# Input tiles normed in pairs, modulation steps of four narrow products, and separate gate and branch entries in a two-layer mixer trunk

## The chip, the cores and the metric

The kernel runs on one core of one Trainium2 chip. A core has five engines with an instruction stream each: TensorE (PE in the profile; PEld is its weight load), VectorE (DVE), ScalarE (ACT), GpSimd (POOL) and SyncE (SP, which issues the transfers). The metric is the device time of one execution in microseconds (us).

## The reference, cut to what matters

Two layers work on 512 latent tokens and 256 context tokens, 1024 channels wide. Each layer modulates a normed input, sends it through one wide projection to three branches (a gated delta rule, RG-LRU, neighbourhood attention), gates and merges the branches, and adds the projected sum back.

```python
for l in range(DEPTH):
    shift_l, scale_l, gate_l = jnp.split(silu_c @ w_mod[l] + b_mod[l], 3, axis=-1)
    shift_c, scale_c, gate_c = jnp.split(silu_cc @ w_mod[l] + b_mod[l], 3, axis=-1)
    h_lat = rms_norm(x, g_pre[l]) * (1.0 + scale_l[:, None]) + shift_l[:, None]
    h_ctx = rms_norm(ctx, g_pre[l]) * (1.0 + scale_c) + shift_c
    y_lat, y_ctx = hybrid_mixer(h_lat, h_ctx, ...)
    x = x + gate_l[:, None] * rms_norm(y_lat, g_post[l])
    if not last:
        ctx = ctx + gate_c * rms_norm(y_ctx, g_post[l])
# in hybrid_mixer:
p_lat, p_ctx = h_lat @ w_in, h_ctx @ w_in      # 3 branches' inputs, gates z, merge gates
merged = (gates[..., 0, :] * (ya @ w_branch[0])
          + gates[..., 1, :] * (yb @ w_branch[1])
          + gates[..., 2, :] * (yc @ w_branch[2]))
return merged @ w_out
```

## The kernel before, in words

**Tiling.** The 768 tokens are six tiles of 128: tiles 0 to 3 are latent, 4 and 5 context. The normed and modulated input `h` is kept transposed (channels on partitions) as a pair of fp16 halves, high and low. A weight chunk of 128 output columns arrives in fp32 in a ring of three raw buffers (`raw_t`), ACT casts its high half (`whi_...`), DVE subtracts to get the low half (`wlo_...`), and each chunk is then 24 matmuls of 512 latent columns (high by high, high by low, low by high over eight blocks of channels) and, where the context needs it, 24 of 256. A branch chunk (`b`) has half as many.

**Order.** Generators write the program. A planner, `Flow`, resumes whichever generator it holds ready by its own estimates of times, and so fixes a written order for each engine; on the chip every engine follows that order strictly. The main generator of a layer walks through the tokens of `schedule(l)` (L208): the inputs of the delta rule (`a`) and of attention (`k`, `q`, `v`), the branch gates (`z`, `za`, `zb`), the RG-LRU inputs (`xb`), the merge gates (`g`, each followed at once by its branch chunk `b`), and `("out",)`, at which the output weights are requested. Background generators (the delta rule, RG-LRU, attention, merging) fill in between. In the traces the projection of token `g` in layer 1 is called `1_g`, and the first three chunks of a layer, whose tokens are taken early, are called `f`, `f1`, `f2` (with `c` for context).

**Modulation.** `silu(c)` and `silu(c_ctx)` are the two real columns of the 32-column stationary operand `sc`. One part of a layer's `w_mod` is 8 steps: a 512 KB transfer `wm`, then two fp32 products of 512 columns into `pm` (L483), each in one group of 32 PSUM partitions. The steps run one at a time between projections. Parts 0 and 1 (shift and scale) of layer 1 are computed in layer 0's `g` 2 phase, part 2 (the output gate) of each layer in its `g` 0 phase by `gate_rows` (L534). All take their `wm` buffers from the same ring of three as the weight chunks. For layer 0 the startup computes shift and scale in four quarters of 256 columns (`pmq`, L667), each a 2 MB piece of `w_mod`.

**Startup.** `startup` (L587) fetches constants, the six input tiles `xt`, one weight chunk, quarter 0 of `w_mod`, two more chunks and quarters 1 to 3. Tiles are squared on ACT and scaled on DVE in a group of two and a group of four (`tiles_`, L632), transposed in fp32 (`xTp`, L266), and when all are transposed, `quarter` 0 starts, then 1 to 3 after one another; each gives shift and scale (`sa`, `sb`) for a quarter of the channels, `h` for them, and a quarter of the products `f`.

**RG-LRU and out stage.** `rg_core` (L861) runs one chain for each of four `j` (conv, two block-diagonal products `lru`, gates, scans on DVE), and yields `yb`, on which the branch products `b` 1 wait. After the merge, `out_tiles` (L1540) multiplies the merged pair `mg` by the output weights (`py`, 48 products of 512 columns for a tile), and `out_tail` (L1493) norms each tile, adds the residual and, in layer 0, squares and norms again (`normed`, L568), transposes (`xTp` from `sq`) and writes `h` for layer 1. A tail does its additions only when the tails before the previous one have ended, and its transposes only when the previous one has.

Of the kernel before, what the change touches and what calls it, by code (L numbers as in the profile page):

```python
# [17 lines left out]
P = 128  # L18
D = 1024
# [188 lines left out]
def schedule(l):  # L208
# [25 lines left out]
def build(tc, A, out):  # L234
# [133 lines left out]
    class Weights:  # L368


        def __init__(self):
            self.seq, self.raw, self.pair, self.more, self.n = [], [], [], None, 0
            for l in range(DEPTH):
                for t in schedule(l):
                    if len(t) > 1:
                        self.seq.append((A["w_in"][l, chunk_of(t)], KD, (l,) + t))
                    if t[0] == "g":
                        self.seq.append((A["w_branch"][l, t[1], t[2]], 4, (l, "b") + t[1:]))
# [94 lines left out]
    def mod_rows(l, part, fin, load):  # L473


        nxt_ = load(l, part, 0)
        yield nxt_
        pm = pst(f"pm{l}_{part}", [P, 512], keep=True)
        for k in range(KD):
            raw = nxt_  # L480
            for n in range(2):
                g = 32 * (2 * n + k % 2)
                nc.tensor.matmul(pm[g:g + 32, :], sc[:, k, :], raw[:, n, :], start=k < 2, stop=k >= KD - 2,  # L483
                                 tile_position=(0, g))
            fl.product(pm, 1.02)
            fl.drop(raw)
            fl.used[raw.name] = fl.now
            if k < KD - 1:
                nxt_ = load(l, part, k + 1)
                yield nxt_  # L490
# [37 lines left out]
    def wload(l, part, k):  # L528
        raw = raw_t([P, 2, 512], "wm")
# [4 lines left out]
    def gate_rows(l, pp, out_, rowt):  # L534
# [26 lines left out]
        yield from mod_rows(l, 2, fin, wload)  # L561
# [6 lines left out]
    def normed(pp, xt, dst=None):  # L568

        jk = pp.tile([P, D], F16, tag="jk", name="jk")  # L570
        ss = small.tile([P, 2], F32, tag="nss", name="nss")
        for i, hf in enumerate((slice(0, 512), slice(512, D))):
            S.activation(jk[:, hf], xt[:, hf], AF.Square, accum_out=ss[:, i:i + 1])
# [4 lines left out]
        sq = dst if dst is not None else pp.tile([P, D], F32, tag="xo", name="sq", bufs=4)  # L578
# [8 lines left out]
    def startup(mod, firsts):  # L587


        with tc.tile_pool(name="n0", bufs=1) as pp:  # L590
# [32 lines left out]
            fl.spawn(lru_rates(), 0)  # L623
# [8 lines left out]
            def tiles_(ts):  # L632

                n_ = len(ts)
                ss = pp.tile([P, 4, 2], F32, tag="xss", name="xss", bufs=6)[:, :n_]
                r = pp.tile([P, 4], F32, tag="xr", name="xr", bufs=6)[:, :n_]
                for i, t in enumerate(ts):
                    yield fl.until(xts[t])
                    for n in range(2):
                        jk = pp.tile([P, 512], F16, tag="jk", name="jk")  # L640
                        S.activation(jk, xts[t][:, n * 512:(n + 1) * 512], AF.Square, accum_out=ss[:, i, n:n + 1])
# [3 lines left out]
                rsqrt(r, ss[:, :, 0], n_, "l4")  # L645
                for i, t in enumerate(ts):
                    V.tensor_scalar(xts[t], xts[t], r[:, i:i + 1], None, op0=OP.mult)
                for t in ts:
                    yield fl.until(xts[t])
                    for q in range(2):  # L650
# [4 lines left out]
                        copy(xT[:, 4 * q:4 * q + 4, t * P:(t + 1) * P], pt)  # L655

            def quarter(q, before):
                yield before
                yield from fl.room()
                pm = pst("pmq", [P, 256], keep=True)  # L660
                for k in range(KD):
                    raw = raws[q, k - k % 2]
                    if k % 2 == 0:
                        yield fl.until(raw)
# [4 lines left out]
                    fl.product(pm, 0.5)  # L669
                row = pp.tile([P, 256], F32, tag="row", name="row")  # L670
                S.activation(row, pm, AF.Copy)
                fl.drop(pm)
                yield fl.until(row)
# [3 lines left out]
                for s, sl in enumerate((slice(0, SEQ), slice(SEQ, NT))):  # L677
                    if s == 1:
                        pass
                    for k in (2 * q, 2 * q + 1):  # L680
                        (V, G)[s].tensor_scalar(xT[:, k, sl], xT[:, k, sl], mod["sa"][:, k, s:s + 1],
                                        mod["sb"][:, k, s:s + 1], op0=OP.mult, op1=OP.add)
# [4 lines left out]
            xt_ = [fl.spawn(tiles_(ts), 1) for ts in ((0,1),(2,3,4,5))]  # L687
            ready, begun = {}, set()
# [11 lines left out]
            ws = []  # L700
            for wn in firsts:
                ws.append((yield from W.take(wn)))
            os_ = [pair_t("f0"), (lat_t("f1"), pst("f1c", [P, CTX], keep=True)),
                   (pst("f2", [P, SEQ], keep=True), pst("f2c", [P, CTX], keep=True))]
            for q in range(4):
                ks = (2 * q, 2 * q + 1)
                for s in range(2):
                    yield lambda: (q, s) in ready
                    yield ready[q, s] - fl.now
                    for w, o in zip(ws, os_):  # L710
# [27 lines left out]
    def layer(l, mod, first):  # L738
# [309 lines left out]
        def merge_in(mp, mg, br, m, o, t, first_, final, before):  # L1048
# [8 lines left out]
            if final:  # L1057
# [5 lines left out]
                                       op0=OP.mult, op1=OP.subtract)  # L1063

# [428 lines left out]
        def out_tail(pp, t, py, xt, gg, h, nmod, before):  # L1493

            jk = pp.tile([P, D], F16, tag="jk", name="jk")
            ss = small.tile([P, 2], F32, tag="nss", name="nss")
            for hf in range(2):
                S.activation(jk[:, hf * 512:(hf + 1) * 512], py[hf], AF.Square, scale=1.0 / SW,
# [5 lines left out]
            yield ended(*before[:-1])  # L1504
            xo = pp.tile([P, D], F32, tag="xo", name="xo", bufs=4)
            for hf in range(2):
# [3 lines left out]
                V.tensor_tensor(xo[:, cols], xo[:, cols], xt[:, cols], OP.add)  # L1510
# [313 lines left out]
```

## Time and profile before

| | |
|---|---|
| median of 3 runs | 1702.24 us (1702.2 to 1704.13) |
| the profiled execution | 1702.02 us, of which its span 1700.3 us |
| mean granted TensorE clock | 0.992 |
| PE busy | 1628.7 us, 96% of the span |
| PEld, DVE | 1026.5 us (60%), 1203.6 us (71%) |
| ACT, POOL | 886.9 us (52%), 270.1 us (16%) |
| moved | 139.80 MB, mean 82 GB/s |

The span is that of the engines' first to last instruction; what lies around it is 1.72 us. Busy times are shares of one execution; they overlap between engines. PE is busy nearly throughout, so the sums in the text count the time that it waits and the work that it does.

### The profile page before, as it was taken

The page shows a single profiled execution, that of the slowest core. Times are in us where ns is not written, and L with a number is a line of the kernel's source. Part 1 is how long each engine was busy: PE and PEld are TensorE (multiplying, and loading weights), DVE is VectorE, ACT ScalarE, POOL GpSimd, SP SyncE. Part 2 cuts the span into 40 slices and gives each one's busy share as a digit, 9 for nine tenths or more (in the row PEclk, how much of TensorE's full clock was granted, in tenths as well). Part 3 has the DMA queues.
Part 4 walks back from the last instruction along what each step waited for, and adds up shares of the span by engine and source line. Part 5 has one row for each costly group of instructions (what it writes and reads, how often), then busy time and mean ns, then how long its engine had stood idle before and what let it go on. Part 6 is the DMA issues. An engine that isn't in the chain of part 4 may idle for free. (4 is left out here: it accounts for less than half of the span.)

```text
span 1700.3 us, 30340 instructions
## 1 busy us (share of the span) xinstructions
PE 1628.7 (96%) x11452; PEld 1026.5 (60%) x11452; DVE 1203.6 (71%) x2866; ACT 886.9 (52%) x2130; POOL 270.1 (16%) x420
## 2 busy tenths in 40 slices
PE   5999999999999999999999899999999999999998
PEld 3666877766667655555655455677756666543443
DVE  5577888775877647785544657988777998677754
ACT  5345665555555426652333545766555666666431
POOL 0003120001322001131220001322003220122210
PEclk9999999999999999999999999999999999999999
DMA  9221111111222232233432102211121112334532
GB/s 360 60 63 55 40 44 44 39 60 40 76 76 69 92 113 69 87 111 113 130 112 81 62 26 77 68 37 34 57 74 45 57 38 82 99 118 124 170 109 75
DMA packets 48387, 139.80 MB, mean 82 GB/s; under 512 B 8048, under 2 KB 8688, under 8 KB 48240
## 3 DMA queue, kind: packets, MB, share of 16 engines
q1 hardware_dynamic: 48240, 137.86, 25.3%
q8 instruction: 90, 1.47, 0.4%
q14 instruction: 57, 0.47, 0.1%
HBM read 133.64 MB, written 4.19 MB: 81 GB/s over the span
## 5 line engine op out<-in xcount | busy, mean ns | idle before, releaser
L262 PEld LDWEIGHTS <-whi_g 128*128 128x128 f16 x1152 | 107.9, 98 | 83.1 <-issue 5.9
L199 DVE SCALAR_TENSOR_TENSOR wlo_g<-raw,whi_g 128x512 f16<-128x512 f32 x96 | 101.5, 1097 | 11.2 <-ACT whi_g L199 11.1
L262 PE MATMUL py<-wo,mg 128*128 128x512 f16 x480 | 104.9, 379 | 0.0
L199 ACT ACTIVATE X<-px 128x256 f16<-128x256 f32 x175 | 65.8, 383 | 62.9 <-PE px L262 59.1
L262 PEld LDWEIGHTS <-whi_a 128*128 128x128 f16 x704 | 69.1, 99 | 47.1 <-issue 5.2
L262 PE MATMUL 1_g<-h,whi_g 128*128 128x512 f16 x384 | 93.7, 379 | 0.0
L262 PE MATMUL 0_g<-h,whi_g 128*128 128x512 f16 x384 | 92.0, 379 | 0.0
L199 DVE SCALAR_TENSOR_TENSOR coa<-cba,cva,coa 128x770 f32<-128x770 f32 (+1 forms) x72 | 71.3, 990 | 24.2 <-ACT coa L199 23.0
L199 ACT ACTIVATE di<-py 64x128 f16<-64x128 f32 x241 | 64.8, 271 | 44.2 <-PE py L262 21.6
L262 PEld LDWEIGHTS <-whi_b 128*128 128x128 f16 x576 | 53.5, 98 | 45.5 <-issue 6.2
L262 PEld LDWEIGHTS <-mg 128*128 128x128 f16 x480 | 46.9, 98 | 55.1
L262 PEld LDWEIGHTS <-wlo_g 128*128 128x128 f16 x576 | 54.2, 98 | 37.8
L199 POOL TENSOR_SCALAR_AFFINE_SELECT dec<-dec 128x256 f32<-128x256 f32 x48 | 24.5, 517 | 316.6 <-ACT dec L199 295.6
L199 POOL MEMSET cba<- 128x2 f32 (+1 forms) x72 | 3.7, 99 | 432.5 <-DVE coa L199 371.3
L199 ACT ACTIVATE whi_g<-raw 128x512 f16<-128x512 f32 x96 | 54.9, 622 | 25.6 <-DMA raw<-in_w_in 25.5
L199 DVE TENSOR_TENSOR ic<-pp,lmc 128x128 f16<-128x128 f32 x240 | 65.2, 283 | 3.6 <-PE pp L262 0.9
L199 POOL TENSOR_TENSOR gm<-trir,gst 128x256 fp32r<-128x256 f32 x96 | 64.0, 693 | 1.0
L199 DVE SCALAR_TENSOR_TENSOR wlo_b<-raw,whi_b 128x512 f16<-128x512 f32 x48 | 36.8, 767 | 35.9 <-ACT whi_b L199 35.8
L262 PEld LDWEIGHTS <-di 128*128 128x128 f16 x480 | 40.7, 98 | 30.3 <-issue 10.3
L199 DVE CAST di<-py 64x128 f16<-64x128 f32 x143 | 40.9, 286 | 24.9 <-ACT di L199 20.8
L199 POOL TENSOR_TENSOR ix<-ix,zz 128x1536 f32<-128x1536 f32 x8 | 27.9, 3489 | 179.5 <-ACT zz L199 179.5
L262 PE MATMUL pp<-X,ld 128*128 128x64 f16 x480 | 52.2, 192 | 2.4 <-ACT oa L199 0.5
(654 smaller groups left out, 4399.7 us busy)
## 6 DMA issues: line engine op xcount, KB each, us to landing
raw<-in_w_in SPq DMA_DIRECT2D x128, 512.0 KB, 3.6
wm<-in_w_mod SPq DMA_DIRECT2D x48, 512.0 KB, 3.7
raw<-in_w_branch SPq DMA_DIRECT2D x48, 256.0 KB, 2.7
rwo<-in_w_out SPq DMA_DIRECT2D x16, 512.0 KB, 3.7
xt<-in_xin SPq DMA_DIRECT2D x12, 512.0 KB, 5.0
bias<-in_rpb SPq DMA_DIRECT2D x24, 256.0 KB, 2.8
lw<-in_lru_w SPq DMA_DIRECT2D x8, 256.0 KB, 3.5
x<-xo SPq DMA_DIRECT2D x4, 512.0 KB, 2.9
```

The costliest lines, as they stand in the source:

```text
L199: return real(*args, **kw)
L262: nc.tensor.matmul(dst, lhsT, rhs, **kw)
```

## The change

- Startup: the first two input tiles are fetched ahead of the constants, and the parameter `lam` after all tiles. Tiles are normed in three pairs; the odd tile of pairs 0 and 2 is squared on DVE, and the odd tile of every pair is scaled on POOL. Quarter 0 of `w_mod` is no longer held until all tiles are transposed; `lru_rates`, some twenty small operations, starts 45 planner microseconds later.
- `w_mod` is laid out so that a step is four products of 256 columns on four groups of 32 partitions. The bytes are the same, and so is the number of steps, 32.
- `gate_rows` gets two buffers of its own, and its steps begin at the second `xb`/`zb` token rather than at `g` 0.
- `g` and `b` are tokens of their own; the order of `xb` and `zb` is turned, and `("out",)` moves behind the first two `g` 1 and `b` 1.
- The out stage: the first tile's products may start per channel block of `merged`; in the tails both halves are transposed together, the chains no longer wait for one another but for transposes written, and squares and additions go by halves. Layer 1's first context products run tile by tile.

```diff
     s += [a1[0], kqv[3][0], a1[1], kqv[3][1], a1[2], kqv[3][2], a1[3], za[0], a1[4], za[1], a1[5], ("merge",)]
-    s += [("g", 2, m) for m in range(KD)] + [za[2], za[3], ("lru",)]
-    for j in range(4):
-        s += [("xb", j), ("zb", j)]
-    s += [("g", 0, m) for m in range(KD)] + [("out",)] + [("g", 1, m) for m in range(KD)]
+    gb = lambda br, ms: [(kind, br, m) for m in ms for kind in "gb"]
+    s += gb(2, range(KD)) + [za[2], za[3], ("lru",)]
+    s += [("zb", 0), ("xb", 0), ("xb", 1)]
+    for j in range(1, 4):
+        s += [("zb", j)] + [("xb", j + 1)] * (j < 3)
+    s += gb(0, range(KD)) + [("g", 1, 0), ("g", 1, 1), ("b", 1, 0), ("b", 1, 1), ("out",)] + gb(1, range(2, KD))
...
-    def mod_rows(l, part, fin, load):
-        nxt_ = load(l, part, 0)
-        yield nxt_
+    def mod_rows(l, part, fin, load, deep=1):
+        ahead = [load(l, part, i) for i in range(deep)]
+        yield ahead[0]
         pm = pst(f"pm{l}_{part}", [P, 512], keep=True)
-        for k in range(KD):
-            raw = nxt_
-            for n in range(2):
-                g = 32 * (2 * n + k % 2)
-                nc.tensor.matmul(pm[g:g + 32, :], sc[:, k, :], raw[:, n, :], start=k < 2, stop=k >= KD - 2,
-                                 tile_position=(0, g))
-            fl.product(pm, 1.02)
+        for i in range(KD):
+            raw = ahead.pop(0)
+            half, kp = i // 4, i % 4
+            for dk in range(2):
+                for n in range(2):
+                    g = 32 * (2 * n + dk)
+                    nc.tensor.matmul(pm[g:g + 32, half * 256:(half + 1) * 256], sc[:, 2 * kp + dk, :],
+                                     raw[:, dk, n, :], start=kp == 0, stop=kp == 3, tile_position=(0, g))
+            fl.product(pm, 0.62)
...
+        def load(l, part, i):
+            t = wp_.tile([P, 2, 2, 256], F32, tag="wm", name="wm", bufs=2)
+            nc.sync.dma_start(t, A["w_mod"][l, part, i])
...
-        yield from mod_rows(l, 2, fin, wload)
+        yield from mod_rows(l, 2, fin, load, 2)
...
+            fetch_x((0, 1))
+            load_first()
+            fl.fetched(cc)
+            fetch_x(range(2, TT))
             for l in range(DEPTH):
                 nc.sync.dma_start(lam[:, l], A["lam"][l])
             fl.fetched(lam)
-            load_first()
-            fl.fetched(cc)
-            fetch_x(range(TT))
...
-            fl.spawn(lru_rates(), 0)
+            fl.spawn(lru_rates(), 6, 45.0)
...
+                        if i == 0 or not vec:
+                            S.activation(jk, half, AF.Square, accum_out=ss[:, i, n:n + 1])
+                        else:
+                            V.tensor_tensor_reduce(jk, half, half, 1.0, 0.0, OP.mult, OP.add,
+                                                   accum_out=ss[:, i, n:n + 1])
...
-                    V.tensor_scalar(xts[t], xts[t], r[:, i:i + 1], None, op0=OP.mult)
...
+                    (V, G)[i].tensor_scalar(xts[t], xts[t], r[:, i:i + 1], None, op0=OP.mult)
...
-            qs, before = [], ended(*xt_)
-            for q in range(4):
-                qs.append(fl.spawn(quarter(q, before), 2))
-                before = ended(qs[-1])
...
+            fl.spawn(quarter(0, lambda: True), 2)
+            fl.spawn(quarter(1, lambda: 0 in summed), 2)
+            fl.spawn(quarter(2, lambda: 1 in summed and (0, 1) in ready), 2)
+            fl.spawn(quarter(3, lambda: 2 in summed and (1, 1) in ready), 2)
...
-            yield ended(*before[:-1])
-            xo = pp.tile([P, D], F32, tag="xo", name="xo", bufs=4)
+            yield lambda: len(turned) >= t - 2
+            xo = pp.tile([P, D], F32, tag="xo", name="xo", bufs=6)
...
-            sq = yield from normed(pp, xo)
-            yield ended(*before)
+            sq = yield from normed(pp, xo, halves)
...
+                if kind in ("xb", "zb") and rp is not None:
+                    if need is not None:
+                        yield fl.until(need)
+                    need = next(side, None)
...
-            yield ended(tails[4], tails[5])
-            for o, w in zip(os_, ws):
-                yield from seg(o[1], SEQ, w, ks, KD, hx, SEQ, NT)
...
+            for t in range(LT, TT):
+                yield ended(tails[t])
+                for o, w in zip(os_, ws):
+                    yield from seg(o[1], SEQ, w, ks, KD, hx, t * P, (t + 1) * P)
```

The next fences are the order written for PE at three places: a row is the line, the operation, out<-in with the shape, and how many follow one another. First, PE from the start of the program, before (`pmt` turns a quarter's result into columns; `f_414` and `f_189` are the first product of layer 0):

```order
L266 MATMUL xTp<-ident,xt 128x128 x48
L667 MATMUL pmq<-wm,sc 32x256 x16
L262 MATMUL pmt_370<-sel_84,row 128x4 x2
L667 MATMUL pmq<-wm,sc 32x256 x16
L262 LDWEIGHTS whi_a
L262 MATMUL f_414<-h_106,whi_a 128x512
```

The same place of the change:

```order
L268 MATMUL xTp<-ident,xt 128x128 x32
L689 MATMUL pmq<-wm,sc 32x256 x16
L268 MATMUL xTp<-ident,xt 128x128 x16
L264 MATMUL pmt_365<-sel_84,row 128x4 x2
L689 MATMUL pmq<-wm,sc 32x256 x16
L264 LDWEIGHTS whi_a
L264 MATMUL f_189<-h_106,whi_a 128x512
```

Quarter 0 has moved ahead of the last 16 transposes; quarter 1 is still ahead of the first `f`. Second, PE at the change of layers, before: the last `py` of layer 0, transposes of tiles 3 and 4, and the first `f` of layer 1.

```order
L262 LDWEIGHTS mg
L262 MATMUL py_11728<-wo,mg 128x512
L266 MATMUL xTp<-ident,sq 128x128 x12
L262 LDWEIGHTS whi_a
L262 MATMUL f_11846<-h_11247,whi_a 128x512
```

The same place of the change:

```order
L264 MATMUL py_11822<-wo,mg 128x512
L264 LDWEIGHTS mg
L264 MATMUL py_11823<-wo,mg 128x512
L264 LDWEIGHTS whi_a
L264 MATMUL f_11941<-h_11302,whi_a 128x512
```

No transpose is left between `py` and `f`: the eight of tile 3 now stand 36 `py` products earlier, the eight of tile 4 behind the first 12 `f`, and the eight of tile 5 sixty matmuls later. Third, PE around the third step of the gate part of layer 1, before:

```order
L262 LDWEIGHTS wlo_g
L262 MATMUL 1_g_1_19818<-h_11247,wlo_g 128x512
L483 MATMUL pm_2_19784<-wm,sc 32x512 x2
L262 LDWEIGHTS whi_b
L262 MATMUL b_0_1_19861<-ya_16276,whi_b 128x512
```

The first step of the same part in the change:

```order
L264 LDWEIGHTS wlo_xb
L264 MATMUL 1_xb_1c<-h_11302,wlo_xb 128x256
L488 MATMUL pm_2_19491<-wm,sc 32x256 x4
L264 LDWEIGHTS whi_zb
L264 MATMUL 1_zb_19498<-h_11302,whi_zb 128x512
```

The steps have moved from between gate and branch chunks to between the RG-LRU inputs, and each is four narrow products.

## Rows read from the trace of the kernel before

**Rows 1.** Windows of 25 us: stretch, length, busy us of each engine, clock, DMA share, GB/s.

```profile
0.00:25.00 25.00, 8.47 (x42) 8.07 (x43) 14.91 (x58) 14.59 (x34) 0.20 (x4) 1.00 0.86 329
25.00:50.00 25.00, 20.94 (x193) 11.05 (x191) 14.67 (x38) 10.11 (x21) 5.14 (x7) 0.86 0.78 295
950.00:975.00 25.00, 17.31 (x87) 9.13 (x86) 17.13 (x56) 13.91 (x38) 0.26 (x6) 0.90 0.18 63
1500.00:1525.00 25.00, 22.78 (x110) 9.44 (x107) 19.44 (x25) 15.59 (x24) 6.76 (x4) 1.00 0.44 143
```

**Rows 2.** What PE waited for, whole span: us in total, times, longest.

```profile
PE xTp L266 <- DVE xt L199: 16.5, 2, 12.6
PE pm L483 <- DMA wm<-in_w_mod: 6.7, 4, 2.2
```

**Rows 3.** Timeline of the startup: start, length (us), engine, work, [idle before].

```profile
0.80 0.85 SPq L608 DMA_DIRECT2D lam<-in_lam  x2
3.12 2.85 SPq L598 DMA_DIRECT2D xt<-in_xin  x6
25.81 1.93 PE L667 MATMUL pmq<-wm,sc 128*32 128x256 f32 x32
31.91 0.38 PE L262 MATMUL f<-h,whi_a 128*128 128x512 f16 x1 [1.19 <-ACT h L199]
66.55 0.38 PE L262 MATMUL f2c<-h,wlo_a 128*128 128x256 f16 x2
```

**Rows 4.** Timeline of PE: third and fourth quarter of f begin here.

```profile
55.06 1.03 PE L262 MATMUL f<-h,whi_a 128*128 128x512 f16 x4
60.91 1.03 PE L262 MATMUL f<-h,whi_a 128*128 128x512 f16 x4
```

**Rows 5.** Timeline: scaling by sa and sb on POOL in the startup.

```profile
29.73 2.21 POOL L199 TENSOR_SCALAR xT<-xT,sa,sb 128x256 f32<-128x256 f32 x2 [29.23 <-DVE sa L199]
36.89 1.36 POOL L199 TENSOR_SCALAR xT<-xT,sa,sb 128x256 f32<-128x256 f32 x2 [4.95 <-DVE sa L199]
```

**Rows 6.** Groups by line: modulation steps, busy us, mean ns of one, idle before.

```profile
L483 PE MATMUL pm<-wm,sc 128*32 128x512 f32 x128 | 33.7, 605 | 6.7 <-DMA wm<-in_w_mod 6.7
```

**Rows 7.** Timeline of PE: two modulation steps and what follows one.

```profile
599.87 1.05 PE L483 MATMUL pm<-wm,sc 128*32 128x512 f32 x4 [1.68 <-DMA wm<-in_w_mod]
...
1513.25 1.05 PE L483 MATMUL pm<-wm,sc 128*32 128x512 f32 x4 [2.22 <-DMA wm<-in_w_mod]
1514.24 3.63 PE L262 MATMUL 1_g<-h,whi_g 128*128 128x512 f16 x16
```

**Rows 8.** Timeline at the change of layers: PE, and one tile's chain on ACT and DVE.

```profile
955.58 9.23 PE L262 MATMUL py<-wo,mg 128*128 128x512 f16 x42
957.85 0.61 ACT L199 ACTIVATE jk<-xo 128x512 f16<-128x512 f32 x1
961.22 0.75 DVE L199 TENSOR_SCALAR sq<-xo,nr 128x1024 f32<-128x1024 f32 x1
961.88 0.75 DVE L199 SCALAR_TENSOR_TENSOR xo<-py,nr,gg 128x512 f32<-128x512 f32 x1
964.64 1.04 PE L266 MATMUL xTp<-ident,sq 128*128 128x128 f32 x8
973.37 1.09 PE L266 MATMUL xTp<-ident,sq 128*128 128x128 f32 x4 [7.69 <-DVE sq L199]
974.25 4.57 PE L262 MATMUL f<-h,whi_a 128*128 128x512 f16 x15
```

**Rows 9.** Timeline of layer 1: end of the RG-LRU chain and its first consumer.

```profile
1561.61 0.27 PE L262 MATMUL lru<-xh,lw 128*128 128x256 f16 x1
1587.50 0.69 DVE L199 SCALAR_TENSOR_TENSOR yb<-hh,yb 128x512 f16<-128x512 f32 x1 [0.70 <-ACT yb L199]
1592.80 1.89 PE L262 MATMUL b<-yb,whi_b 128*128 128x512 f16 x8
```

**Rows 10.** What SP's queue of weight loads waited for: us in total, times, longest.

```profile
SPq L384 <- PE pm L483: 40.7, 11, 8.6
```

More of the change, by code (lines that the diff above doesn't have):

```diff
@@ L577, in normed @@
         tile_rstd(ss[:, 0:1], r, 1.0 / D, "n")
-        sq = dst if dst is not None else pp.tile([P, D], F32, tag="xo", name="sq", bufs=4)
+        sq = pp.tile([P, D], F32, tag="xo", name="sq", bufs=6)
         V.tensor_scalar(sq, xt, r, None, op0=OP.mult)
@@ L630, in startup, with tiles_ @@
             V.tensor_copy(ident16, ident)
[L632 to L641, printed above, removed]
+            turned = set()
+            def tiles_(ts, vec):
+                ss = pp.tile([P, 2, 2], F32, tag="xss", name="xss", bufs=3)
+                r = pp.tile([P, 2], F32, tag="xr", name="xr", bufs=3)
+                for n in range(2):
+                    for i, t in enumerate(ts):
+                        yield fl.until(xts[t])
+                        jk = pp.tile([P, 512], F16, tag="jk", name="jk", bufs=2)
+                        half = xts[t][:, n * 512:(n + 1) * 512]
+                        if i == 0 or not vec:
[3 more added lines that the diff above has]
+                                                   accum_out=ss[:, i, n:n + 1])
                 yield fl.until(ss)
@@ L655, in tiles_ @@
                         copy(xT[:, 4 * q:4 * q + 4, t * P:(t + 1) * P], pt)
+                        turned.add((t, q))
             def quarter(q, before):
                 yield before
+                for k in range(0, KD, 2):
+                    yield fl.until(raws[q, k])
                 yield from fl.room()
@@ L699, in startup @@
             fl.spawn(splits(), 3)
-            ws = []
-            for wn in firsts:
-                ws.append((yield from W.take(wn)))
+            ws, firsts = [], list(firsts)
             os_ = [pair_t("f0"), (lat_t("f1"), pst("f1c", [P, CTX], keep=True)),
@@ L709, in startup @@
                     yield ready[q, s] - fl.now
-                    for w, o in zip(ws, os_):
+                    for i, o in enumerate(os_):
+                        if i == len(ws):
+                            ws.append((yield from W.take(firsts[i])))
+                        w = ws[i]
                         p, sl = both(o)[1 - s]
@@ L1510, in out_tail @@
                 V.tensor_tensor(xo[:, cols], xo[:, cols], xt[:, cols], OP.add)
+                halves.append(fl.free["dve"])
                 if last:
@@ L1515, in out_tail @@
             if last:
+                turned.append(t)
                 return
@@ L1564, in out_tiles @@
             return h, tails
-        nxt, read = {}, set()
+        merged, gated = {}, {}
+        nxt, read, turned = {}, set(), []
         with ExitStack() as layer_:
@@ L1611, in layer @@
                     need = next(side, None)
+                if kind == "b":
+                    br, m = tkn[1:]
+                    y = (ya, yb, yc)[br]
+                    if br == 1:
+                        yield core
+                    o = yield from proj(4, lambda part, k, a, b: y[:, k, part, a:b], not last, f"b{l}_{br}_{m}",
+                                        (l,) + tkn, br != 2)
+                    sums[m] = fl.spawn(merge_in(mp, mg, br, m, o, gated.pop((br, m)), br == 2, br == 1,
+                                                ended(*([sums[m]] if m in sums else []))), 5)
+                    if m == KD - 1:
+                        for need in side:
+                            if need is not None:
+                                yield fl.until(need)
+                        need = None
+                    continue
                 if kind == "xb" and tkn[1]:
                     lwr = load_lw(tkn[1])
+                if kind in ("xb", "zb") and rp is not None:
+                    if need is not None:
+                        yield fl.until(need)
+                    need = next(side, None)
                 wide = kind in ("k", "v", "xb") or (kind == "a" and tkn[2] != "q") or not last
@@ L1668, in layer @@
                     fl.drop(*[p for p, _ in both(o)])
[L1669 to L1681 removed]
+                    gated[br, m] = t
             if not last:
                 W.ahead()
[L1684 removed]
+            yield ended(*nxt["puts"])
             h, tails = yield from out_tiles(op, mg, nxt["wo"], nxt["gg"], nxt)
```

120 lines of the change are left out of this document (61 added, 59 removed).

## The prediction

> **What bounds the kernel now.** The table has PE busy for 96% of the span, so I read first where the rest is, in windows of 25 us. PE falls short in the startup, at the change of layers and in the gate part of layer 1 [rows 1]: it is busy for 8.47 of the first 25 us and 20.94 of the next, for 17.31 at 950 to 975, and for 22.78 at 1500 to 1525. In two of these stretches the granted clock is low as well, a mean of 0.86 and 0.90. The list of PE's waits names two of the causes: 16.5 us for the normed input tiles, and 6.7 us, four times, for a step of `w_mod` to land [rows 2]. Everywhere else PE works through its written order with hardly a gap, so that there a change counts only by the PE work that it removes or by a wait that it makes. The timelines of the three stretches [rows 3, 4, 7, 8, 9] show what stands ahead of PE in each.
>
> **Modulation steps.** All 32 steps of `pm` change from two products of 512 columns to four of 256. A step now takes 33.7/32 = 1.05 us [rows 6], and the projection behind it starts 0.99 us after it [rows 7], so 0.06 us overlaps with what follows. Four narrow products on four groups are not in the trace as a step by themselves; the nearest rows are the quarters of the startup, 16 products of 256 columns on the same four groups in 1.93 us, which is 0.48 us for four [rows 3]. That is the lower end, since a row of 16 hides its own fill. The group counts two records for a product, so a step has 4 records now and 8 after; 31 starts between the 32 records of the quarter, with a last record of about 0.4 us (a mean of 0.605 for the wide ones [rows 6]), leave (1.93 - 0.38)/31 = 0.05 us from start to start. A lone step is then 7 x 0.05 + 0.38 = 0.73 us, less the same 0.06 of overlap 0.67. The saving is 0.32 us by that and 0.51 by 0.48; I take 0.36, nearer to the lone step, as the steps stand alone between projections. 32 x 0.36 = **11.5 us** (10.2 to 16.3).
>
> **Waits for the steps.** Of the four waits for `wm`, 6.7 us, the one at 599.87 ends part 1 of the modulation in layer 0 with 1.68 us [rows 2, 7]. It takes its buffer from the same ring as before, and the order around it is that of before; it stays. The other three, 6.7 - 1.68 = 5.0 us with 2.22 at 1513.25 the longest, are in the gate part of layer 1, where a step follows on a gate or branch chunk while the ring of three is full of weights. There the change has two buffers for `wm` alone, requests two steps ahead, and its steps stand in the `xb` and `zb` phase, whose projections take longer than a branch chunk. **-5.0 us** (0 to -5.0). The buffer pool that it needs was there before; its price is on SP, among the rivals.
>
> **Startup.** The first `f` begins at 31.91 and the last ends at about 66.55 + 0.22 = 66.77 [rows 3]. A quarter of it without disturbance takes 60.91 - 55.06 = 5.85 us [rows 4], four 23.4; the 34.9 us that it took contain two `pmq` (3.9 us), about 3.5 us lost to the clock, (1 - 0.86) x 25 [rows 1], and small waits for `h`. Ahead of `f` stood 48 transposes, which began only when the tiles were normed [rows 2], then quarters 0 and 1. Now quarter 0 is ahead of the last 16 transposes, so that its columns are there when these end. What is late next is the data: six tiles, three weight chunks and the eight `w_mod` pieces of quarters 0 and 1 are 17 x 0.524 MB (512 KB) = 8.9 MB, at 329 GB/s [rows 1] 27 us from the start, and 24 to 25 if the tiles' requests go from 3.12 up to 0.80, where `lam` stood [rows 3]. Quarter 1 is still ahead of `f` in PE's order, and only the products of the last piece are left when that lands, so `f` can start at about 25.7. From there 23.4 + 3.9 for the last two quarters + an estimated 1 for turning them into columns and 0.9 of wait for quarter 2's data + 3.4 for the clock = 32.6, which ends at 58.3. The gain is 66.77 - 58.3 = **8.5 us**; it falls to 5 if the data of quarter 1 comes at 27 and quarter 2 has to be waited for longer, and rises to 11.4 if most of the clock's loss goes too.
>
> The odd tile is scaled on POOL. It has done such an operation on 128x256 in 1.36/2 = 0.68 us, and in 2.21/2 = 1.1 beside DVE work [rows 5]; four times as many elements are 2.7 to 4.4 us, where DVE needs 0.75 for 128x1024 [rows 8]. This would sit in the chain of the tiles; I cost it at nothing, because the work that hides it is the transfer of quarter 1, which lasts to 24.4, while all tiles were turned before 25.81 even in a group of four [rows 3], and come some 3 us earlier in pairs with shared squares and the first requests ahead; without that cover it costs 2 to 3.6 us, once, for the pair that is late. The Trainium skill (SBUF — State Buffer, section on who interferes with whom) says that DVE and GpSimd hold a shared port pair exclusively, so that the later of the two is blocked. The two POOL rows, 2.21 against 1.36, agree with it; by the page alone the pairs would end later by the whole 0.85 us and more, still inside the same cover.
>
> **Change of layers.** Before, PE ended `py` at 964.8, did eight transposes of `sq`, waited 7.69 us for the next tile's `sq`, and began `f` of layer 1 at 974.25; the 15 matmuls there took 4.57 us where 15 x 0.216 = 3.24 would do at the full clock (0.216 is 9.23/42, less the last one's tail) [rows 8]. After, `f` stands directly behind `py`, with twelve matmuls for tiles 0 to 2 ahead of the next transposes. From the end of a tile's `py` to its `sq` the chain is squares and ten small operations, 961.22 - 957.85 = 3.37 us, four operations by halves at 0.75, and the squares, the small ones and the scaling again, 4.12; that is 10.5 us, or some 10.2 with squares beside additions. PE has sixty matmuls, 13 us, between two tiles' transposes, so each tile fits with 2 to 3 us to spare, if the chains of two tiles don't stand in each other's way on DVE. The saving is 7.69 + 0.7 for the start behind it + 1.3 of slow clock - some 1 us that tile 3's `h` may be late = **8.5 us** (5 to 9.5).
>
> **RG-LRU's tail in layer 1.** The last `lru` products of the chain were at 1561.61, `yb` was written by 1588.2, and the first branch product on it stood at 1592.80: 26.6 us of chain, 4.6 us of slack [rows 9]. The steps and waits that vanish shorten the time ahead of this consumer, and in the new order only five chunks are left behind the last `lru` products: `b` 6, `g` 7, `b` 7 and `g` 1 0 and 1, which is 3 x 24 + 2 x 12 = 96 matmuls of 0.216, or 20.7 us, and about one more of what is left of `g` 6. Against a chain of 26.6 that would cost 4.8 us; but part of the 26.6 was the chain's queueing behind other DVE work, which has time when it is asked for earlier. I take **+1.5 us** (0 to 5).
>
> **The rest.** Between 437 and 590 us and in layer 1's delta rule the planner writes another interleaving, since its estimate of a step has changed; PE waits there are small, so 0, give or take 4. The end of the kernel keeps its tail: 0.
>
> Sum: -11.5 - 5.0 - 8.5 - 8.5 + 1.5 = -32.0. The profiled execution took 1702.02 us, 0.22 below the median of the runs; 1702.0 - 32.0 = **1670.0 us**, and the median of runs should lie as close.
>
> **Rivals.**
> - The startup stays bound by its data, and PE, which then does little ahead of `f`, runs slow for longer. For it: 0.86 of DMA share and the 0.86 clock in the next stretch [rows 1]. The Trainium skill (TensorE: Matmul & The Clock Gate, part 1) has an idle engine fall to half clock and come back when busy, which agrees with these clocks. Worth 5 of the 8.5: 1675. Chance 0.14.
> - RG-LRU becomes the bound in layer 1, since 21.7 us of PE work stand against 26.6 of chain: +5 to +8 instead of +1.5, 1674 to 1677. Against it: with a request earlier, the chain may have less to queue for. Chance 0.13.
> - Better: a lone step costs 0.48, -16.3 instead of -11.5, the chain doesn't stall and the startup loses less to the clock: about 1657. Chance 0.07.
> - Slower than before: SP issues in order, and its weight loads waited 40.7 us in all, 11 times, for a `pm` product to free a raw buffer, at most 8.6 [rows 10]. With `wm` in two buffers of its own a request can stand on SP ahead of the loads of `xb` and `zb` until a step far down PE's order is done. PE's order has a step in every `xb`/`zb` chunk, so that a request is short of a wait; it decides only from 32/16 = 2 us lost by PE at each of the 16 steps of the gate parts: 1704 and more. Chance 0.04, with a re-ordered delta rule.
>
> The forecast itself has 0.62: all four savings there within their bounds, 1661 to 1678. From 1655 (below the better case) to 1684 (two of the shortfalls, each at its end, and the unknown of the re-ordering) it leaves out no more than 2 in 10. A difference of 0.2%, 3.4 us, is about what a measurement of this kernel tells from none; all cases but the last are faster by more: 0.95, and 0.01 and 0.04.
>
> **What would show it.** Right: `f` of layer 0 from about 25.7 and its end at 58 to 59; `pm` steps about 0.7 us apart from what follows; no wait for `wm` in layer 1 but the one near 600 kept; no PE gap of over 1 us at the change of layers and a clock near 1 there; `yb` in layer 1 at most 2 us behind PE. Wrong: a PE wait on `yb` of 5 us or more; a startup that still ends beyond 62; SP waits of the loads on `pm` that grow and weights that come late in the `xb` phase.

## The result, and the profile after

The changed kernel takes 1683.99 us (median of 4 runs, 1680.36 to 1684.91) against 1703.18 before (4 runs): a ratio of 0.9884, 95% interval 0.9872 to 0.9896. That is 19.2 us faster where 32 were forecast; the median lies at the very upper end of the range, which ends at 1684, and two of the four runs (1684.22 and 1684.91) lie beyond it. The profiled execution has a span of 1682.0 us, 18.3 less than before.

The page's first part for the changed kernel:

```profile
span 1682.0 us, 30788 instructions
PE 1616.8 (96%) x11652; PEld 1027.5 (61%) x11652; DVE 1206.9 (72%) x2896; ACT 877.9 (52%) x2107; POOL 279.5 (17%) x423
```

PE's share has not moved. Windows of the changed kernel, which answer to [rows 1] (the third holds the change of layers, the last the first gates of layer 1):

```profile
0.00:25.00 25.00, 10.73 (x72) 8.35 (x73) 12.97 (x50) 12.94 (x29) 11.35 (x7) 1.00 0.94 361
25.00:50.00 25.00, 22.07 (x195) 12.79 (x194) 17.27 (x42) 10.70 (x21) 6.54 (x14) 0.93 0.72 265
940.00:965.00 25.00, 25.00 (x125) 12.41 (x124) 16.55 (x55) 13.76 (x36) 0.40 (x6) 1.00 0.07 22
1485.00:1510.00 25.00, 23.71 (x127) 10.42 (x126) 20.24 (x24) 17.87 (x26) 5.11 (x2) 1.00 0.28 86
```

What PE waited for now, over the span, against [rows 2]:

```profile
PE xTp L268 <- DMA lam<-in_lam: 11.3, 1, 11.3
PE pxt L268 <- DVE Y L199: 7.3, 11, 1.4
...
PE pl L268 <- DVE coa L199: 3.1, 4, 2.3
PE xTp L268 <- POOL xt L199: 3.0, 2, 1.6
PE pm L488 <- DMA wm<-in_w_mod: 2.6, 1, 2.6
...
PE py L264 <- ACT mt L199: 1.5, 1, 1.5
...
PE b L264 <- ACT yb L199: 0.9, 1, 0.9
```

In the third window PE is busy throughout, where it was 17.31 of 25. Two old waits are smaller. POOL's scaling in the startup and `py` at the end are new, and in the delta rule `pxt` (5.0 us before) and `pl` (0.3) have grown (`lam` is only the last thing to land ahead of the first transpose).

To see where the 18.3 us came from, I took the start of the first row of each phase in PE's timelines of both kernels; the length of a phase is the difference between two such starts.

| phase, by PE's first row of it | before | after | difference |
|---|---|---|---|
| startup, to the first `0_z` | 66.76 | 61.57 | -5.19 |
| to `0_g` 2 | 355.45 | 355.73 | +0.28 |
| `g` 2 of layer 0, with 16 steps, to `0_za` | 181.13 | 175.96 | -5.17 |
| to the first `py` (8 steps in it) | 296.52 | 292.37 | -4.15 |
| first `py` to the first `f` of layer 1 | 74.39 | 65.65 | -8.74 |
| `f` of layer 1 to `1_z` | 25.87 | 25.33 | -0.54 |
| `1_z` to `1_g` 2 (delta rule, attention) | 302.65 | 311.79 | **+9.14** |
| `1_g` 2 to `1_za` | 122.77 | 122.74 | -0.03 |
| to the last layer's `py` (8 steps, 3 of the waits) | 224.64 | 219.04 | -5.60 |
| `py` to the end of the last one | 41.60 | 43.27 | +1.67 |

One phase gives half of the gain back: the delta rule of layer 1, in which the change edits nothing.

### The profile page after: what moved, and what is told of

It reads as the page before. It is cut to its first block, busy times and chain, and to the rows that moved or that the text cites. A ratio compares the mean times of both kernels' runs of the same rounds, so it can differ in the third digit from the quotient of the medians.

```text
span 1682.0 us, 30788 instructions
## 1 busy us (share of the span) xinstructions
PE 1616.8 (96%) x11652; PEld 1027.5 (61%) x11652; DVE 1206.9 (72%) x2896; ACT 877.9 (52%) x2107; POOL 279.5 (17%) x423
## 5 line engine op out<-in xcount | busy, mean ns | idle before, releaser
L199 DVE SCALAR_TENSOR_TENSOR wlo_g<-raw,whi_g 128x512 f16<-128x512 f32 x96 | 90.7, 985 | 23.8 <-ACT whi_g L199 23.8
L199 DVE CAST di<-py 64x128 f16<-64x128 f32 x150 | 43.0, 287 | 23.9 <-ACT di L199 15.9
L199 POOL TENSOR_TENSOR mt<-mg,mt 128x768 f32<-128x768 f32 (+1 forms) x16 | 33.1, 2072 | 117.6 <-DVE mt L199 117.6
```

The source lines that it names most:

```text
L199: return real(*args, **kw)
```

## The experiments

**The out tail, and the written order.** Theory A: the change of layers gives its gain back, since PE comes early to chains on DVE and ACT. Theory B, or O below: the planner wrote another order in layer 1, and this order costs the time. First, the old out tail in the changed kernel.

```diff
...
-            yield lambda: len(turned) >= t - 2
+            yield ended(*before[:-1])
...
-            for t in range(LT, TT):
-                yield ended(tails[t])
-                for o, w in zip(os_, ws):
-                    yield from seg(o[1], SEQ, w, ks, KD, hx, t * P, (t + 1) * P)
+            yield ended(tails[4], tails[5])
+            for o, w in zip(os_, ws):
+                yield from seg(o[1], SEQ, w, ks, KD, hx, SEQ, NT)
```

> The changed kernel with the old out stage: tails wait for one another, transposes of tile 4 stand before the first f of layer 1, context products of both tiles at once. In the change the step from py to f gained 8.7 us, and the stretch from the first f to the first 1_g of layer 1 lost 8.6 us (328.5 to 337.1). Theory A (given back: PE reaches layer 1 earlier than the chains on DVE and ACT that feed its delta rule, so the gain turns into waits there): the step costs 8 to 9 again, the stretch returns to 327 to 331, the total stays at 1682 to 1686. Theory B (the stretch lost through another written order, on its own): the step costs 8 to 9 again, the stretch stays at 335 to 339, the total is 1690 to 1694.

Measured: 1683.28 us, ratio 0.9887 (0.9871 to 0.9903), level with the change. The step from `py` to `f` costs 74.38 again, and the stretch from `f` to `1_g` takes 331.7, close to the 327 to 331 of theory A. But PE's written order in the stretch came out row for row that of the kernel before, so this run alone does not tell A from O. Where the two orders part, PE has before:

```
L262 MATMUL 1_z_12185<-h_11247,whi_z 128x512
L266 MATMUL pl_12208<-ident,coa 128x128 x3
L266 MATMUL pl_12209<-ident,coa 128x128 x3
L262 LDWEIGHTS whi_z
L262 MATMUL 1_z_12185<-h_11247,whi_z 128x512
```

and in the change `pl` stands behind all of this `1_z` and more. From there on the two differ in many places: of the 2322 matmul records that either trace has of the stretch, about 70% stand in a common sequence.

Second, an order changed by the planner's price alone:

```diff
-            fl.product(pm, 0.62)
+            fl.product(pm, 1.02)
```

> The changed kernel with the planner's price of a modulation step put back from 0.62 to 1.02 us; the instructions are the same ones, only their written order differs. Theory B (the written order of the delta rule decides): the layer 1 stretch from f to 1_g moves by 3 us or more in some direction from 337.1 and the total by as much, 1676 to 1690. Theory A (given back): the stretch stays within 2 us of 337, the total within 1682 to 1686.

Measured: 1685.94 us, 0.9903 (0.9888 to 0.9918). It tells nothing of the two theories: the price moved rows in layer 0 and late in layer 1, but not in the stretch, which has the change's order and takes 311.7 us. So the new price is not what changed the order there.

So I crossed the two directly. The planner's clock is set back at the start of layer 1, until PE's order in the stretch is that of before, while all instructions are the change's:

```diff
+            fl.free["dve"], fl.free["act"] = fl.now - 6.89, fl.now - 8.23
+            for n_ in list(fl.ready):
+                if fl.ready[n_] > fl.now - 5 and not n_.startswith(("f2c", "raw")):
+                    fl.ready[n_] = fl.now - 5
+            for n_ in list(fl.used):
+                fl.used[n_] = min(fl.used[n_], fl.now - 5)
```

> The changed kernel, new out stage and all, with the planner's clock set back for ACT and DVE by some microseconds where layer 1 begins, so that PE's written order from the first 1_z to the first 1_g is row for row that of the kernel before (the run with the old out tail had that order too, and there and before this stretch took 302.7 and 304.6 us; the four kernels with the new out stage, all with the new order, took 309.4 to 311.8). Theory O (the written order of layer 1 is the cause): the stretch takes 302 to 305 us, the total falls to 1674 to 1680. Theory A (PE comes too early for DVE and ACT, whatever the order): the stretch stays at 308 to 312, the total at 1680 to 1686.

Measured: 1677.25 us, 0.9870 (0.9846 to 0.9894), as theory O. And the counterpart, the old tail with the change's order, by the same means (DVE and ACT free 3.43 and 5.13 us ahead of PE, `f0c` and `f1c` ready 2.55 and 1.18 us ago):

> The counterpart of the run with the old layer 1 order: the old out tail, with the planner's clock for ACT and DVE set where layer 1 begins so that PE's written order from the first 1_z to the first 1_g is row for row that of the change. Theory O (the written order costs the time): this stretch takes 309 to 313 us instead of 304.6 with the old tail and its own order, the total 1689 to 1692. Theory A (what counts is how early PE arrives): the stretch stays at 303 to 306, total 1682 to 1685.

Measured: 1691.58 us, 0.9948 (0.9928 to 0.9967), again O. The windows of the stretch from `1_z` to `1_g`, one for each kernel; before and the old tail's own order:

```profile
1000.12:1302.77 302.65, 296.31 (x2325) 206.27 (x2323) 238.38 (x672) 177.07 (x484) 45.36 (x110) 0.99 0.18 55
```

```profile
985.75:1290.33 304.58, 296.91 (x2324) 206.26 (x2322) 238.83 (x672) 176.70 (x484) 45.52 (x110) 0.99 0.17 55
```

the new tail with the old order:

```profile
976.72:1281.69 304.97, 296.99 (x2325) 206.36 (x2323) 241.30 (x674) 177.77 (x487) 45.50 (x110) 0.99 0.18 56
```

the change, and the old tail with the change's order:

```profile
976.61:1288.40 311.79, 300.53 (x2326) 207.48 (x2323) 245.33 (x678) 175.89 (x483) 43.91 (x110) 0.98 0.18 55
```

```profile
986.17:1296.73 310.56, 299.01 (x2324) 206.73 (x2322) 242.47 (x675) 174.67 (x480) 43.62 (x110) 0.99 0.17 54
```

With the old order the stretch takes 302.7 to 305.0 us, with the new one 310.6 to 311.8, whichever tail stands ahead of it. Between kernels that have the same tail, the order costs 6.0 and 6.8 us; between kernels that have the same order there, the tail costs 0.4 and 1.2.

A part of such differences is the granted clock. Inside the stretch PE runs at half clock (0.50, 1.2 GHz) for 3.4 us in the first two of these traces, for 6.8 in the third, for 10.2 in the change and for 6.8 in the last; at half clock at most half of the time is lost. Traces with the same time at half clock can be compared as they are. At 3.4 us the old order takes 302.7, 304.6 and 304.3 us (the narrow steps alone, below), and 306.3 in the combined kernel with the early request, where PE waits 1.6 us more for a weight; the new order takes 309.4, 309.6 and 309.9 (DVE scaling, the early request and the old startup, below). At 6.8 us the old one takes 305.0, and 304.7 in the combined kernel, the new one 310.6 to 311.1 in three traces. So the order costs 5 to 6 us by itself, and of the 9.1 us of the table up to 3.4 are clock.

PE's waits there (us in total, times, longest), first of the change, then of the new tail with the old order:

```profile
PE pxt L268 <- DVE Y L199: 4.6, 5, 1.4
PE pl L268 <- DVE coa L199: 2.7, 3, 2.3
```

```profile
PE pxt L268 <- DVE Y L199: 2.3, 3, 1.7
PE pl L268 <- DVE coa L199: 1.9, 1, 1.9
```

In the new order the transposes of the delta rule's inverse (`pxt`) come up oftener before DVE has written `Y`.

**The startup.** The old startup in the changed kernel, and the changed one with all scaling on DVE:

> The changed kernel with the old startup. In the change the first product behind the startup began 5.2 us earlier. Theory S1 (all of it is kept to the end): 1688 to 1691, later stretches as in the change within 1 us. Theory S2 (the stretches behind it give some back, or the other order loses or gains): later stretches differ by 2 us or more from those of the change, and the total is outside 1687 to 1691.

Measured: 1688.29 us, 0.9915 (0.9898 to 0.9931). The gain of the startup, 4.3 us by the medians, is kept to the end; only `1_z` to the first `1_k` differs by more than a microsecond (46.9 against 48.2 us), at the same order, and PE was at half clock there for 3.4 us instead of 6.8.

```diff
-                    (V, G)[i].tensor_scalar(xts[t], xts[t], r[:, i:i + 1], None, op0=OP.mult)
+                    V.tensor_scalar(xts[t], xts[t], r[:, i:i + 1], None, op0=OP.mult)
```

> The changed kernel with every startup tile scaled on DVE, none on POOL. In the change POOL took 3.4 to 3.9 us for a tile, and two groups of transposes waited for it, 3.0 us in all. Theory P (POOL's scaling is on the path): f begins 2 to 3.5 us before 29.47, near 26.5, and the total is 1680 to 1682. Theory D (the data of quarter 1 and the columns behind quarter 0 set the start): f begins within 1 us of 29.5, total 1683 to 1685.

Measured: 1679.05 us, 0.9862 (0.9847 to 0.9876). Neither theory alone: `f` begins at 28.00, 1.5 us earlier than in the change. The timeline of the change (start, length, engine, work, [idle before]):

```profile
10.52 3.40 POOL L199 TENSOR_SCALAR xt<-xt,xr 128x1024 f32<-128x1024 f32 x1 [10.02 <-DVE xr L199]
15.67 7.75 POOL L199 TENSOR_SCALAR xt<-xt,xr 128x1024 f32<-128x1024 f32 x2 [1.75 <-issue]
...
19.06 2.82 PE L268 MATMUL xTp<-ident,xt 128*128 128x128 f32 x12 [1.41 <-POOL xt L199]
21.81 2.36 PE L689 MATMUL pmq<-wm,sc 128*32 128x256 f32 x32
24.11 1.97 PE L268 MATMUL xTp<-ident,xt 128*128 128x128 f32 x16
25.91 0.51 PE L264 MATMUL pmt<-sel,row 128*128 128x4 f32 x4
...
29.47 0.38 PE L264 MATMUL f<-h,whi_a 128*128 128x512 f16 x1 [1.19 <-ACT h L199]
```

and with DVE scaling:

```profile
20.01 1.93 PE L689 MATMUL pmq<-wm,sc 128*32 128x256 f32 x32
...
23.68 0.51 PE L264 MATMUL pmt<-sel,row 128*128 128x4 f32 x4
...
26.14 0.64 PE L689 MATMUL pmq<-wm,sc 128*32 128x256 f32 x8 [0.64 <-DMA wm<-in_w_mod]
27.43 0.64 PE L689 MATMUL pmq<-wm,sc 128*32 128x256 f32 x8 [0.65 <-DMA wm<-in_w_mod]
28.00 0.39 PE L264 MATMUL f<-h,whi_a 128*128 128x512 f16 x1
```

POOL holds the tiles back first; without it quarter 1's last piece, landing at about 27.4, is what `f` waits for (at 26.3 in the combined kernel below, where `f` begins at 26.87).

The 1.5 us are not POOL's alone. Six other traces here have this startup unchanged, POOL's scaling included, and begin `f` at 28.23 to 28.46. This is the run with the other price:

```profile
18.90 1.53 PE L268 MATMUL xTp<-ident,xt 128*128 128x128 f32 x12 [1.51 <-POOL xt L199]
20.36 1.93 PE L689 MATMUL pmq<-wm,sc 128*32 128x256 f32 x32
```

In the change the same twelve transposes take 2.82 us and the products of quarter 0 2.36: PE came to its full speed later. The change's trace has no record of the granted clock ahead of 22.7 us, those six none ahead of 17.0 to 18.1, and before none ahead of 24.3, so the 1.00 that a window of the first 25 us shows [rows 1] is no measurement. With DVE scaling `f` begins at 26.87 to 28.00 in three traces (the run above and the two combined kernels below), so that POOL's scaling costs 0.2 to 1.6 us there.

The product behind the startup begins at 59.35 against 61.57, which is 2.2 of the 4.9 us between the medians. To see what the rest is, the change once more beside other kernels:

> The changed kernel itself once more, unchanged, beside the others on one chip. The run with DVE scaling differs from it in three instructions and came out 4.9 us faster in the medians, of which the startup shows 2.2. If the rest is spread between sessions, this comes out at 1680 to 1682; if the scaling does it, at 1683 to 1685.

Measured: 1682.74 us, 0.9895 (0.9879 to 0.9910); its first `0_z` is at 61.47. It lies between the two cases, so some 1.5 us of the difference are neither spread between sessions nor startup. PE's order is the same in both traces from start to end, and the differences stand in two phases (174.6 against 175.9 us in `g` 2 of layer 0, 46.8 against 48.2 between `1_z` and `1_k`). Windows in these two phases, the change first, then DVE scaling:

```profile
580.00:600.00 20.00, 16.66 (x101) 8.82 (x99) 7.20 (x18) 4.40 (x11) 0.00 (x0) 0.83 0.41 131
1000.00:1020.00 20.00, 17.02 (x75) 8.54 (x74) 14.47 (x29) 7.86 (x22) 0.16 (x3) 0.83 0.27 80
```

```profile
580.00:600.00 20.00, 16.72 (x108) 9.00 (x101) 6.46 (x14) 3.73 (x7) 0.00 (x0) 0.91 0.43 132
1000.00:1020.00 20.00, 17.45 (x100) 10.59 (x99) 12.61 (x27) 9.24 (x25) 0.33 (x6) 0.91 0.25 79
```

A granted clock of 0.83 over 20 us is 6.8 us at half clock, 0.91 is about 3.4, and the difference is up to 1.7 us in each window. So what is left is the clock, and not the scaling. Why PE stayed at half clock for longer in one trace, behind nearly the same wait near 590 (2.63 and 2.57 us), stays open.

**The steps.** The narrow steps alone in the kernel before, with the price of before so that PE's order stays:

> The kernel before with only the modulation steps changed (four products of 256 columns on four groups, new layout); the planner's price stays at 1.02, so that the written order is that of before but for the steps. By the steps of the changed profile (0.57 against 0.98 us to what follows) 32 x 0.41 = 13.1 us are saved: 1688 to 1691 if all of it is kept and the waits for wm stay at 6.7 us; 1691 to 1695 if the four waits grow, since PE comes to each step earlier and its transfer does not.

Measured: 1694.07 us, 0.9957 (0.9945 to 0.9969): the second case. The group of steps in that run, and in the change:

```profile
L486 PE MATMUL pm<-wm,sc 128*32 128x256 f32 x256 | 20.4, 391 | 9.6 <-DMA wm<-in_w_mod 9.6
```

```profile
L488 PE MATMUL pm<-wm,sc 128*32 128x256 f32 x256 | 20.9, 399 | 2.6 <-DMA wm<-in_w_mod 2.6
```

and PE's timeline of the change at one step (all single steps of this trace repeat its 0.57 us to what follows, all of before 0.98 or 0.99):

```profile
1456.58 0.64 PE L488 MATMUL pm<-wm,sc 128*32 128x256 f32 x8
1457.15 1.04 PE L264 MATMUL 1_xb<-h,whi_xb 128*128 128x512 f16 x4
```

Without buffers of their own, faster steps wait longer, 9.6 instead of the 6.7 us of [rows 6]: 13.1 - 2.9 = 10.2 us should be left, and 8.6 are, between the medians beside each other (1702.71 and 1694.07). The other 1.6 may be clock: up to the last product its trace is at half clock for 30.6 us in all, that of before for 23.9, which is up to 3.4 us.

The wait that the change keeps, at 589.74, has grown from 1.68 to 2.63 us. In the next run the last two steps no longer stand together, since the leftover ones go to the two `za` projections that follow:

```diff
...
-                if kind in "gb":
+                if kind in "gb" or kind == "za" and tkn[1] > 1:
...
-                    if m == KD - 1:
+                    if m == KD - 1 and br != 2:
```

> The changed kernel with the last modulation steps of layer 0's g 2 phase done at the two za projections behind it, so that the last two steps no longer stand together. In the change the second of them waits 2.63 us for its transfer, the columns behind it 0.7, and the clock of 550 to 600 is 0.93. Theory: the wait and the slow clock go, 3 to 6 us less, 1678 to 1681. Rival: the wait only moves, since the ring of three buffers still feeds weights and steps in turn: 1683 to 1685.

Measured: 1677.79 us, 0.9868 (0.9849 to 0.9886), 5 to 6 us less than the change. Windows of 560 to 600, the change first:

```profile
560.00:600.00 40.00, 36.28 (x292) 22.71 (x291) 20.43 (x55) 14.31 (x43) 0.00 (x0) 0.91 0.36 113
```

```profile
560.00:600.00 40.00, 39.62 (x322) 24.72 (x321) 19.93 (x50) 15.69 (x44) 0.00 (x0) 1.00 0.38 120
```

A wait of 2.6 us and the 0.7 us behind it cost near 6: 3.3 more of idle, and a granted clock of 0.91 over 40 us, up to 3.4 more. The price is not a fixed one: behind nearly the same wait PE was at half clock for 6.8 us in the change and for 3.4 with DVE scaling.

**The request of the output weights** put back ahead of `g` 1, in the change and in a kernel that combines the three improvements above:

```diff
-    s += gb(0, range(KD)) + [("g", 1, 0), ("g", 1, 1), ("b", 1, 0), ("b", 1, 1), ("out",)] + gb(1, range(2, KD))
+    s += gb(0, range(KD)) + [("out",), ("g", 1, 0), ("g", 1, 1), ("b", 1, 0), ("b", 1, 1)] + gb(1, range(2, KD))
```

> The changed kernel with the request of the output weights put back ahead of the first g 1. In the change the casts of these weights on ACT and DVE still run beside the last merges, the tanh of the last g 1 comes late, and the second py product waits 1.51 us for the bank that it reads. Theory W (the late request makes this wait): the wait goes, py to the last product takes 41.6 us as before instead of 43.27, total 1681 to 1683. Rival: with the request ahead of them the first g 1 are held until RG-LRU has ended, and b 1 begins 1 to 5 us later: 1684 to 1688.

Measured: 1686.69 us, 0.9922 (0.9904 to 0.9939). `py` takes 41.60 as before, without the new wait. PE also comes later to `py` here, so that this run alone does not show that the late casts make the wait; the timeline of the change does:

```profile
1627.04 1.22 DVE L199 SCALAR_TENSOR_TENSOR wo<-rwo,wo 128x1024 f16<-128x1024 f32 x1 [1.65 <-ACT wo L199]
1628.78 0.68 DVE L199 SCALAR_TENSOR_TENSOR mt<-mt,b 128x512 f32<-128x512 f32 x1
...
1630.90 0.63 ACT L199 ACTIVATE mg<-mt 128x512 f16<-128x512 f32 x1 [3.37 <-POOL mt L199]
1631.44 0.58 ACT L199 ACTIVATE mt<-1_g 128x512 f32<-128x512 f32 x1
```

The products of `b` 6 ended at 1622.4, but their merge on DVE (`mt<-mt,b`) stands in DVE's order behind the cast of the output weights (`wo`), which waits 1.65 us for ACT. POOL's part of the merge, ACT's `mg` and the last tanh (`mt<-1_g`) follow one another, and `py` goes on at 1632.07. In the run with the early request the cast is gone from there; but the first `b` 1 begins 2.3 us later relative to `1_g` 0, and from 1480 on PE waits where it did not:

```profile
PE b L264 <- ACT whi_b L199: 5.0, 3, 2.2
```

That is neither theory W as a whole nor the rival's cause: it is not RG-LRU that comes late, but branch weights, whose cast waits.

> The changed kernel with all startup tiles scaled on DVE, the old written order in layer 1's delta rule, and the last modulation steps deferred. If the three add up: 5 for the scaling (1679.05 against 1683.99), 6 for the order, 3 to 6 for the steps, 1667 to 1671. If the order brings nothing (theory A): 1673 to 1677.

Measured: 1667.80 us, 0.9812 (0.9794 to 0.9830): DVE scaling, the old order in layer 1 and the deferred steps add up, to the fastest version here, 16 us below the change (15 below its second measurement).

> The combined kernel (tiles scaled on DVE, old layer 1 order, last modulation steps deferred; 1667.8 us) with the output weights requested ahead of the first g 1. Theory W: 1665.5 to 1667. Rival: 1668 to 1672.

Measured: 1673.27 us, 0.9840 (0.9824 to 0.9856): 5.5 us slower than without, even beyond the rival's 1672, and with the same waits for branch weights.

## Why the prediction was right or wrong

The time came out within the range, but by luck: the range ends at 1684, and the median is 1683.99. All four savings came within their bounds, which was the condition of the forecast's own case, and yet the time is not in its 1661 to 1678, because most of the gain that is missing was lost at terms put at 0.

- **Modulation steps** (11.5): right, mis-sized by little. A step takes 0.64 us end to end, and what follows starts 0.57 behind it (1456.58 to 1457.15) against 0.98; 32 x 0.41 = 13.1 us. The price from the quarters' start-to-start time plus one fill, 0.73, was too high by 0.09.
- **Waits for the steps** (5.0): right for layer 1, where none is left; the one kept in layer 0 grew by 0.95 us, since faster steps reach the same transfer sooner, as the narrow steps alone show (2.65 us at the same place).
- **Startup** (8.5): 5.2 in this trace; six others with the same startup end it at 60.3 to 60.6, some 1.1 us earlier. From `f` on the forecast holds (32.6 us, measured 32.10), so what failed stands ahead of `f`: 29.47 instead of 25.7. First, the nothing for POOL's scaling. One tile took 3.4 us and two took 7.75, inside the 2.7 to 4.4 us worked out from [rows 5], but the cover, quarter 1's data, was not what PE waited for: the transposes and quarter 0 stand in order ahead of it, and `pmt` came at 25.91. From there the columns, `sa`, and `h` took 3.6 us more, as they did before (28.25 to 31.91), and the prediction left them in the shadow of quarter 1. Second, the data: where DVE does the scaling, quarter 1's last piece is the limit, at 26.3 to 27.4 and not at the 24.4 worked out. Therefore taking POOL out gives 0.2 to 1.6 us at `f`, and not the 2 to 3.6 that the prediction gave without the cover. Third, some 1.1 us of PE at its lower speed in this trace.
- **Change of layers** (8.5): right, 8.74, with PE busy throughout and the clock at 1.00.
- **RG-LRU's tail** (+1.5): right, PE waits for `yb` 0.9 and 0.4 us. The 21.7 us of PE work behind the last `lru` are there (1554.89 to 1576.58), and the chain took 24.7 us and not 26.6, as the prediction thought possible.
- **The rest** (0, give or take 4): this is the step that failed most. The stretch behind `1_z` lost 9.1 us, of which 5 to 6 come from the planner's other order there and up to 3.4 from more time at half clock in this trace. What set it off was not the new price of a step, as the prediction had it, but the new tails, by which the planner's clock has DVE and ACT free 3.43 and 5.13 us ahead of PE when layer 1 begins, and not 6.89 and 8.23 as with the old tails; the crossed runs set these numbers and so the order. It was costed from the idle time of before, which says what PE loses in one order and nothing of another.
- **The end** (0): 1.67 us lost; 1.51 of it is the second `py` product, which waits for the last tanh. The late casts of the output weights make this wait, by the chain shown above, and with the early request it is gone.

Of the total, 9.1 + 3.3 + 1.7 = 14.1 us too much was forecast in three places, another 0.95 for the wait that is kept, and 1.6 too little for the steps; the sum of 13.4 us is nearly all of the 13.7 us between a span of 1682.0 and the forecast 1668.3 (1700.3 - 32.0).

## What to carry to other kernels

Where a planner writes the order, a change in one stage can rewrite a later one that it does not touch: compare the order of every later stretch, not only of the edited one, and where it changed, put the old order back by hand to price it. An engine named as cover must be the one waited for: follow the chain of the covered step to its first consumer in the written order before costing it at nothing. A request that is moved has to be weighed against every transfer and cast that it passes; here both places of the output weights make a wait, and the later one is cheaper. And before a microsecond or two between traces is put down to an edit, the granted clock of both has to be read, stretch by stretch.

## What the hardware showed unexpectedly

POOL scaled a tile of 128x1024 in 3.4 to 3.9 us where DVE took 0.75 [rows 8]; the planner's price for it was n/1000 + 0.12, or 1.14 us. A wait of 2.63 us near 590 was followed by a clock of 0.91 over a window of 40 us, so that taking it away gave about twice its length. PE was at half clock for 3.4 us in some traces and 6.8 in others, in the same phase and with the same PE order, and the length of such a phase differs by 1 to 1.5 us with it. The spread between runs of one kernel goes the same way: of 13 runs of the kernel before, the shortest, 1697.21 us, had a mean granted clock of 0.994, the longest, 1705.31, one of 0.989. What decides how long PE stays at half clock is not shown here.
